# Seven-product groups in the last piece's down projection, 37 of them in the up projection, and mixer A's values in fp32r

## The chip, the cores and the metric

The kernel runs on one core of a Trainium2 chip. The metric is the device time of one execution, in microseconds. Three runs of the kernel before took 1312.78, 1313.6 and 1313.22 us; their median is 1313.22.

## The reference

One layer of a hybrid diffusion backbone, for 128 context tokens and 128 latent tokens, in fp32, model width 2048. Both token groups use the same weights. Each sub-layer is modulated by shift, scale and gate, which come from a conditioning vector.

```
m = silu(c) @ w_ada + b_ada              -> shift1, scale1, gate1, shift2, scale2, gate2
h = rmsnorm(x)*(1+scale1) + shift1
q,k,v of mixer A (8 heads, 2 kv heads), q,k,v of mixer B (8 heads), gates gA, gB = h @ w_in
oA = softmax(qA kA' + sink) vA           # latent tokens also see 128 cached context keys
oB = softmax(qB kB' + bias) vB           # 2-D neighbourhood, and the cached keys
x = x + gate1*((sig(gA)*(oA @ w_br_a) + sig(gB)*(oB @ w_br_b)) @ w_out)
h2 = rmsnorm(x)*(1+scale2) + shift2
x = x + gate2*(relu(h2 @ w_up)**2 @ w_down)   # 2048 -> 8192 -> 2048
```

The outputs are the two x and the new keys and values. Of these steps the change touches `probs @ vA` of mixer A, `h2 @ w_up`, and the last eighth of the sum over 8192 in `@ w_down`.

## The kernel before, in words

**Products.** An fp32 matmul is done as three fp32r products: with x = xH + xL and w = wH + wL, it is xH wH + xH wL + xL wH. A weight tile of 128 x 1024 (512 KB) is loaded by a DMA on SyncE's queue (`raw`), ScalarE copies the high half into `wH` (helper L112), VectorE subtracts, `wL = raw - wH` (L272), and TensorE does twelve matmuls of 128x512 with it, about half of them for context, half for latent tokens.

**Order.** The kernel records a list of steps, `wsteps`, one per weight tile. `run()` goes through them: for each step it issues the loads that are due (the digits of `RUN` say how many steps ahead), prepares the high and low halves as many steps ahead as `LOOK` says (`AHEAD` for high halves alone), issues the step's matmuls, and then whatever was put behind that step with `at(step, function)`: attention jobs, transposes, sums. On each engine the order is then fixed. SyncE's queue holds loads, transposing DMAs and stores in order. POOL's queue holds DMAs that add to a tile: `minus_plus` (L279) makes a low half by writing -wH with ScalarE and adding the weights from memory, in place of VectorE's subtraction, for the steps that `LO_DMA`, `XL_DMA`, `YL_DMA` list; `T_DMA` lists groups one of whose sums is made in the same way (L1477). Large tiles come from one pool of `GEN` buffers of 128 x 1024 fp32. Accumulators are banks: four in `pacc`, four in `paux`.

**MLP.** It runs in 8 pieces of 1024 hidden columns. A piece is first computed (`up_unit` for piece 0, `up_pair` for the others), then relu, square and transposition, then four down units of 512 output columns, each of four steps with twelve matmuls. They add up in `dsum` from piece to piece; a unit begins with a bank that holds the sum so far (`seed`). In the last piece the units end with the gate, the residual and the store (L1145, L1149, L1583); the very last unit, `last_unit`, ends in smaller parts.

**Seven products.** `up_pair(p)` goes through 8 groups of the inner dimension, two weight tiles each. A group multiplies a 2x2 block of inputs with a 2x2 block of weights. A plain group does the eight block products with 24 matmuls. A group that `FAST[p]` lists does it with seven products (Strassen and Winograd's scheme), 21 matmuls into banks `Q1` to `Q7`; plain groups add to some of the same banks and to `Z`. For a seven-group VectorE and ScalarE form sums of weight blocks and split them all: `XH, XL`, `YB` (both halves), `tH, tL`, `uH, uL`. The sums of inputs, `sH, sL`, are made once, by `fast_stat`. At the end of a pair VectorE adds the banks into the results (L1552).

**Mixer A's values.** `values()` (L991) multiplies the transposed probabilities with v in plain fp32, one matmul of 512 columns (four heads) per block of keys: two jobs of one block (context), two of two blocks (latent). The probabilities are transposed by a DMA and joined again (`probs_join`), for the jobs that `TE` lists by TensorE (L970).

**Constants.** `load_consts` loads the rope table, three norm weights and the sink by five DMAs.

## Time and profile before

| | |
|---|---|
| median of 3 runs | 1313.22 us |
| profiled execution: its own time / its span | 1312.65 us / 1310.8 us |
| TensorE busy (matmul) | 1303.2 us, 6333 records |
| TensorE weight loads, beside the matmuls | 1057.9 us |
| VectorE / ScalarE / GpSimd busy | 1126.5 / 904.5 / 57.4 us |
| DMA | 400.90 MB, 306 GB/s in the mean |
| granted clock of the profiled execution | 0.999 |

The span is that of the instructions in the profile; the 1.85 us between it and the execution's own time lie around them. "Busy" of TensorE counts from a matmul's start to its modelled end, and consecutive ones overlap. Rows of groups read: line, engine, operation, output<-inputs, shapes, count, then busy us and mean ns, then the idle time of the engine ahead of them and what ended it. Rows of a timeline begin with start and duration in us; in square brackets stands the idle time before, with its releaser.

### The profile page before, as it was taken

Reading aid. Unit: us, or ns where it says so; the run is one execution under the profiler, and the core shown is the slowest. Engines: PE = TensorE matmul, PEld = TensorE weight load, DVE = VectorE, ACT = ScalarE, POOL = GpSimd, SP = SyncE. Lnnn points to the kernel's source line nnn. Section 1 sums busy time; section 2 is a strip of 40 time slices with the busy share of each in tenths; the row PEclk is TensorE's granted clock in tenths of the full one; section 3 lists DMA queues with packets and bytes.
Section 4 is the critical chain, followed back from the end, with each engine's and each line's share of the span. In section 5 each row is a group of like instructions: output and inputs, shape, how many; then the busy total and the mean of one; then the engine's idle time right before and its main releaser. Section 6 shows DMA issues by size and latency. Waiting matters only on the chain.

```text
span 1310.8 us, 17957 instructions
## 1 busy us (share of the span) xinstructions
PE 1303.2 (99%) x6333; PEld 1057.9 (81%) x6334; DVE 1126.5 (86%) x1446; ACT 904.5 (69%) x1145; POOL 57.4 (4%) x66
## 2 busy tenths in 40 slices
PE   9999999999999999999999999999999999999998
PEld 4778788788788878888888888888888888888887
DVE  4669799989999899999778998987999998789663
ACT  5635566699865655636786878859779597696980
POOL 0000000332000000000000000000000000000000
PEclk9999999999999999999999999999999999999999
DMA  9999999897999989997599789779977978869593
GB/s 371 408 409 408 400 409 389 346 321 232 271 347 349 386 294 365 359 334 235 205 300 318 204 269 287 275 269 273 322 240 238 362 245 278 301 205 367 193 355 96
DMA packets 170138, 400.90 MB, mean 306 GB/s; under 512 B 71840, under 2 KB 73088, under 8 KB 170048
## 3 DMA queue, kind: packets, MB, share of 16 engines
q1 hardware_dynamic: 165744, 387.36, 82.3%
q0 software_dynamic: 4160, 12.32, 5.0%
q8 instruction: 49, 0.80, 0.2%
q14 instruction: 41, 0.34, 0.1%
q10 hardware_dynamic: 144, 0.08, 0.1%
HBM read 373.97 MB, written 10.80 MB: 294 GB/s over the span
## 4 chain that ended last, share of the span: by engine, by line
PE 98%; ACT 1%; DMA 1%; SPq 0%; issue 0%; DVE 0%; ACTq 0%
PE acc L347 17%; PE acc L348 17%; PE acc L349 17%; PE Q L1421 6%; PE Q L1420 6%; PE Q L1419 6%; PE acc L474 5%; PE acc L475 5%; PE acc L476 5%; PE ps_ada L365 3%; PE ps_S L920 1%; PE Z L1421 1%; PE Z L1420 1%; PE Z L1419 1%; DMA araw<-in_w_pair 1%; PE acc L1225 1%
## 5 line engine op out<-in xcount | busy, mean ns | idle before, releaser
L272 DVE TENSOR_TENSOR wL<-raw,wH 128x1024 fp32r<-128x1024 f32 x377 | 442.7, 1219 | 51.2 <-ACT wH L112 49.0
L112 ACT ACTIVATE wH<-raw 128x1024 fp32r<-128x1024 f32 (+1 forms) x394 | 388.5, 1039 | 62.3 <-DMA raw<-in_w_in 22.6
L474 PE MATMUL acc<-wH,hH 128*128 128x512 f32 x272 | 107.1, 394 | 0.6 <-ACT srow L112 0.6
L475 PE MATMUL acc<-wL,hH 128*128 128x512 f32 x272 | 105.9, 389 | 0.0
L476 PE MATMUL acc<-wH,hL 128*128 128x512 f32 x272 | 105.9, 389 | 0.0
L347 PE MATMUL acc<-wH,hH 128*128 128x512 f32 x252 | 101.2, 402 | 0.0
L348 PE MATMUL acc<-wL,hH 128*128 128x512 f32 x252 | 98.3, 390 | 0.0
L349 PE MATMUL acc<-wH,hL 128*128 128x512 f32 x252 | 98.2, 390 | 0.0
L1685 DVE CUSTOM_DVE_ANT_0 aT<-aT,cB,cols 128x1024 f32<-128x1024 f32 x56 | 71.4, 1283 | 0.6
L1685 DVE CUSTOM_DVE_ANT_0 junk<-aT,cB,cols 128x1024 bf16<-128x1024 f32 x56 | 71.2, 1279 | 0.0
L112 ACT ACTIVATE uH<-raw 128x1024 fp32r<-128x1024 f32 x34 | 36.1, 1062 | 47.4 <-DVE raw L1514 38.2
L474 PEld LDWEIGHTS acc<-wH,hH 128*128 128x128 f32 x272 | 51.0, 188 | 14.2 <-issue 2.9
L476 PEld LDWEIGHTS acc<-wH,hL 128*128 128x128 f32 x272 | 51.1, 188 | 10.8
L475 PEld LDWEIGHTS acc<-wL,hH 128*128 128x128 f32 x272 | 51.1, 188 | 10.2
L347 PEld LDWEIGHTS acc<-wH,hH 128*128 128x128 f32 x252 | 47.4, 188 | 10.6 <-issue 1.0
L348 PEld LDWEIGHTS acc<-wL,hH 128*128 128x128 f32 x252 | 47.4, 188 | 10.5 <-issue 0.7
L349 PEld LDWEIGHTS acc<-wH,hL 128*128 128x128 f32 x252 | 47.3, 188 | 9.9
L112 ACT ACTIVATE tH<-t 128x1024 fp32r<-128x1024 f32 x31 | 32.8, 1058 | 30.4 <-DVE t L1506 26.2
L112 ACT ACTIVATE fTa<-pTa 128x2048 uint16<-128x2048 uint16 x16 | 40.5, 2533 | 1.3 <-DVE gc_g L1685 1.3
L1685 DVE CUSTOM_DVE_ANT_0 aT<-aT,cB,gc_g 128x1024 f32<-128x1024 f32 x32 | 40.7, 1282 | 0.4
L1685 DVE CUSTOM_DVE_ANT_0 junk<-aT,cB,gc_g 128x1024 bf16<-128x1024 f32 x32 | 40.7, 1280 | 0.0
L1562 ACT ACTIVATE up<-up 128x1024 f32<-128x1024 f32 x28 | 29.7, 1062 | 15.4 <-DVE up L1552 14.9
(694 smaller groups left out, 3351.9 us busy)
## 6 DMA issues: line engine op xcount, KB each, us to landing
raw<-in_w_in SPq DMA_DIRECT2D x131, 512.0 KB, 9.0
raw<-in_w_down SPq DMA_DIRECT2D x128, 512.0 KB, 6.8
araw<-in_w_pair SPq DMA_DIRECT2D x80, 512.0 KB, 9.8
raw<-in_w_upF SPq DMA_DIRECT2D x68, 512.0 KB, 6.3
aT<-in_w_gT SPq DMA_DIRECT2D x64, 512.0 KB, 7.1
raw<-in_w_up SPq DMA_DIRECT2D x60, 512.0 KB, 6.8
aT<-in_w_adaT SPq DMA_DIRECT2D x48, 512.0 KB, 8.0
raw<-in_w_out SPq DMA_DIRECT2D x32, 512.0 KB, 7.8
```

The source lines that it names most:

```text
L112: act.activation(out, in_, AF.Copy)
L272: dve.tensor_tensor(st["lo"], st["raw"], st["hi"].bitcast(F32), op=OP.subtract)
L347: pe.matmul(acc[tb], sh, wh[:, k, :], start=f, stop=False, **kw)
L348: pe.matmul(acc[tb], sh, wl[:, k, :], start=False, stop=False, **kw)
L349: pe.matmul(acc[tb], sl, wh[:, k, :], start=False, stop=l, **kw)
L474: pe.matmul(acc[tb], sh, wh[:, k, :], start=kt == 0 and k == 0 and not held and not seeded, stop=False, **kw)
L475: pe.matmul(acc[tb], sh, wl[:, k, :], start=False, stop=False, **kw)
L476: pe.matmul(acc[tb], sl, wh[:, k, :], start=False, stop=last and k == 1 and not hold, **kw)
L1419: pe.matmul(acc, stat[0], hi, start=f, stop=False)
L1420: pe.matmul(acc, stat[0], lo, start=False, stop=False)
L1421: pe.matmul(acc, stat[1], hi, start=False, stop=l)
L1685: dve.tensor_tensor_reduce(out, box["raw"], cB[s, tag], 1.0, dst if second else baT[:, part, fb:fb + 1], OP.mult, OP.add, dst)
```

## The change

Five things, beside the tables.

1. **Last piece, down units 1 and 2.** They become a pair, `down_pair`, in the manner of an up pair: four groups, of which `FAST_D = (0, 3)` are groups of seven, both from the first half of the piece (`a14`); the two plain ones are those of the second half (`a15`). `up_pair` becomes a caller of a general `pair()`. The banks `Q2, Q4, Q3, Z` begin with the sums of the earlier pieces, copied in three steps ahead (`sown`). `up_T` keeps the joined values of these two hidden tiles, and `stat_sums` makes the sums of inputs for both of them, though the groups of seven read those of `a14` alone. A new input, `w_downF`, holds the weights of these two units in the arrangement of the seven products. Gate, residual and stores of both units come after the pair.
2. **`FAST` lists 37 groups in place of 34**: pairs 1, 3 and 7 have one more, so pairs 3 and 7 have six and the others five.
3. **Mixer A's values** are three fp32r products per block. VectorE and ScalarE split v once (`values_split`) and the probabilities of each job (`probs_split`).
4. **`TE` lists one more job**, a latent one of mixer A: its probabilities are transposed on TensorE, eight transposes in place of a DMA.
5. **Constants in two loads**, from one array `consts`. With smaller tiles for small vectors and less memory for DMA descriptors, there are 54 large buffers in place of 53.

The tables that set the order are all new: `RUN`, `LOOK`, `AHEAD`, and the places of attention jobs, transposes and accumulating DMAs (POOL's rise from 26 to 38). One gate tile in place of two goes to memory and back, and seven sums in place of eight. `G2_LEAD`, 2 before and -3 now, puts the last loads of gates and residuals behind the last weight loads.

The diff's core:

```diff
-GEN = 53
-SCRATCH = 4096
+GEN = 54
+SCRATCH = 1024
...
-TE = (('A', 0, 1), ('qA', 1), ('qB', 1))
+TE = (('A', 0, 1), ('A', 1, 1), ('qA', 1), ('qB', 1))
...
-G2_LEAD = 2
+G2_LEAD = -3
...
-FAST = {1: (0, 1, 5, 7), 2: (0, 2, 3, 5, 7), 3: (0, 2, 3, 5, 7), 4: (0, 1, 3, 6, 7), 5: (0, 1, 3, 5, 7), 6: (0, 1, 3, 5, 7), 7: (0, 1, 3, 5, 7)}
+FAST = {1: (0, 1, 2, 3, 7), 2: (0, 2, 3, 6, 7), 3: (0, 1, 2, 3, 5, 7), 4: (0, 2, 4, 5, 7), 5: (0, 3, 5, 6, 7), 6: (0, 1, 3, 4, 7), 7: (0, 1, 2, 4, 6, 7)}
...
+V_AT = 75
+SOW_AT = 3
+FAST_D = (0, 3)
+DS_AT = [-12, -1]
...
+    def values_split():
+
+        t = [G(f"v{x}A", F32R)[:, 0:768].rearrange("p (b g d) -> p b g d", b=3, g=2) for x in "HL"]
+        new = units["kvA", 0][:, :, 256:512].rearrange("p s (g d) -> p s g d", g=2)
+        for b, src in ((slice(0, 2), new), (2, K2["ca"][:, 1])):
+            copy(t[0][:, b], src)
+            dve.tensor_tensor(t[1][:, b], src, t[0][:, b].bitcast(F32), op=OP.subtract)
+        vA["hl"] = t
...
+        def probs_split():
+            if mix == "A":
+                t = [G(f"P{x}", F32R)[:, 0:n // 2].rearrange("p (b h q) -> p b h q", b=nb, h=4) for x in "HL"]
+                split(t[0], t[1], st.pop("PT"))
+                st["PH"] = t
...
             if mix == "A":
+                vh, vl = vA["hl"]
                 for b in range(nb):
-                    pe.matmul(ps, v(0, b), st["PT"][:, b].rearrange("p h q -> p (h q)"), start=b == 0, stop=b == nb - 1)
+                    j = 2 if b else s
+                    for i, (x, y) in enumerate(((vh, 0), (vh, 1), (vl, 0))):
+                        pe.matmul(ps, x[:, j, g, :], st["PH"][y][:, b].rearrange("p h q -> p (h q)"),
+                                  start=b == 0 and i == 0, stop=b == nb - 1 and i == 2)
...
+    def down_pair(n0, n1):
+
+        units = PIECES[last]
...
+        def done(n, u):
+            g, r = gbc["g2", n], x1[n]
+            dve.tensor_tensor(u, u, g, op=OP.mult)
+            dve.tensor_tensor(r, r, u, op=OP.add)
+            for s in range(2):
+                out_dma(n, s)
+
+        def sown():
+            return [(q, dsum[n][:, s, :]) for q, n, s in (("Q2", n0, 0), ("Q4", n0, 1), ("Q3", n1, 0), ("Z", n1, 1))]
+
+        for i, n in enumerate(units):
+            at(len(wsteps) + DS_AT[i], lambda n=n: stat_sums(dH, dL, n, aF.pop(n)))
+        pair(len(PIECES), n0, n1, ("down", last, n0), a["w_down"], 4 * units[0], a["w_downF"], FAST_D, 4, x, sc, done, sown)
...
-        for n in range(4):
-            down_unit(p, n)
+        if p < last:
+            for n in range(4):
+                down_unit(p, n)
+        else:
+            down_unit(p, 0)
+            down_pair(1, 2)
+            down_unit(p, 3)
```

**How the order changes, in three places.** On TensorE, in the input projection, at a job of mixer A's values of two blocks (`hH`, `hL` are the halves of h; before):

```order
L347 MATMUL acc<-wH,hH_261 128x512
L348 MATMUL acc<-wL,hH_261 128x512
L349 MATMUL acc<-wH,hL_262 128x512
L991 MATMUL ps_o<-fTPA_3375,u_kvA_2025 128x512
L991 MATMUL ps_o<-fTPA_3375,cacheA 128x512
L347 MATMUL acc<-wH,hH_261 128x512
```

and a job of one block in the changed kernel, with the new transposes behind it:

```order
L353 MATMUL acc<-wH,hL_761 128x512
L1018 MATMUL ps_o<-PH,vHA 128x512
L1018 MATMUL ps_o<-PL,vHA 128x512
L1018 MATMUL ps_o<-PH,vLA 128x512
L986 MATMUL ps_PT<-ident,prob 128x128 x8
L936 MATMUL ps_S<-fTkB_3439,T_qB_3442 128x128 x4
L351 MATMUL acc<-wH,hH_760 128x512
```

One product per block has become three; the eight transposes (`ps_PT`) stand between values and the scores of mixer B (`ps_S`).

On TensorE in the last piece, where unit 1 began before and the pair begins now. Before, a plain step follows a plain step (`a14`, `a15` are the two halves of the piece):

```order
L348 MATMUL acc<-wL,a15H 128x512
L349 MATMUL acc<-wH,a15L 128x512
L347 MATMUL acc<-wH,a14H 128x512
L348 MATMUL acc<-wL,a14H 128x512
L349 MATMUL acc<-wH,a14L 128x512
```

Now unit 0 is followed by the pair's first group of seven and its first plain group:

```order
L353 MATMUL acc<-wH,a15L 128x512
L1479 MATMUL Q_11617<-XH,a14H 128x512
L1480 MATMUL Q_11617<-XL,a14H 128x512
L1481 MATMUL Q_11617<-XH,a14L 128x512
...
L1479 MATMUL Q_11619<-tH,sH_11324 128x512
L1480 MATMUL Q_11619<-tL,sH_11324 128x512
L1481 MATMUL Q_11619<-tH,sL_11325 128x512
...
L1479 MATMUL Q_11538<-wH,a15H 128x512
L1480 MATMUL Q_11538<-wL,a15H 128x512
L1481 MATMUL Q_11538<-wH,a15L 128x512
```

Between the first and the second triple stand twelve matmuls, into the second free bank of `pacc` and into three of the banks begun with copied sums, so `Q_11619`, the first of the banks that unit 0 used, is written from the 16th matmul on.

On SyncE's queue, the end. Before (`g` and `x1b` are the gate and residual rows of a unit; `x1d` is where the residual was kept):

```order
L243 DMA raw<-in_w_down 128x1024 x4
L1711 DMA g_2_11461<-gr_g_10605 128x512 x2
L1330 DMA x1b_11464<-x1d_6239 128x1024
L243 DMA raw<-in_w_down 128x1024 x2
L1583 DMA out_y_prompt<-x1b_11263 128x512
L1583 DMA out_y_sample<-x1b_11263 128x512
L1711 DMA g_3_11554<-gr_g_10605 128x512 x2
L1330 DMA x1b_11557<-x1d_6258 128x1024
```

Now:

```order
L247 DMA raw<-in_w_downF 128x1024
L247 DMA raw<-in_w_down 128x1024 x3
L1635 DMA out_y_prompt<-x1b_11422 128x512
L1635 DMA out_y_sample<-x1b_11422 128x512
L247 DMA raw<-in_w_down 128x1024
L1798 DMA g_1_11664<-gr_g_10640 128x512 x2
L1364 DMA x1b_11667<-x1d_6275 128x1024
L1798 DMA g_2_11683<-gr_g_10640 128x512 x2
L1364 DMA x1b_11686<-x1d_6289 128x1024
```

The last weight load has moved behind the output stores of unit 0 (`x1b_11422`), and the gate and residual rows of units 1 to 3 have moved behind it.

167 lines of the change are left out of this document (101 added, 66 removed).

## The prediction

> **What bounds the kernel now.** I read the busy times first, then the chain of waits, then what TensorE itself waited for. In the rows of the page below the shares are of the 1310.8 us span; the second row is the chain that ended last, by engine.
>
> ```profile
> PE 1303.2 (99%) x6333; PEld 1057.9 (81%) x6334; DVE 1126.5 (86%) x1446; ACT 904.5 (69%) x1145; POOL 57.4 (4%) x66
> PE 98%; ACT 1%; DMA 1%; SPq 0%; issue 0%; DVE 0%; ACTq 0%
> ```
>
> TensorE is busy for all but 7.6 us, and the chain runs through it. TensorE's list of waits has five entries, none over 1.2 us; the first and the last are these (columns: us in total, times, longest):
>
> ```profile
> PE ps_warm L136 <- DVE wm L129: 1.2, 1, 1.2
> ...
> PE ps_warm L136 <- issue: 0.2, 1, 0.2
> ```
>
> Together they come to 3.3 us, all on lines of the first stage, ahead of anything that the change touches. So from there on the time is the number of TensorE instructions times their pitch. The timeline gives the pitch:
>
> ```profile
> 1186.16 0.39 PE L1419 MATMUL Q<-tH,sH 128*128 128x512 f32 x1
> ...
> 1188.43 0.39 PE L1420 MATMUL Q<-uL,sH 128*128 128x512 f32 x1
> ```
>
> Ten fp32r matmuls of 512 columns lie between these two starts: 2.27/10 = 0.227 us each (the 0.39 is a latency that overlaps the next). VectorE is the engine nearest to taking over. Three stretches show how near, and that the granted clock is full (columns: us, then busy time of PE, PEld, DVE, ACT, POOL with counts, granted clock, DMA share, GB/s):
>
> ```profile
> 310.00:560.00 250.00, 250.00 (x1199) 204.99 (x1198) 240.17 (x325) 164.97 (x207) 0.00 (x0) 1.00 0.95 334
> 1100.00:1190.00 90.00, 90.00 (x399) 74.43 (x398) 78.31 (x87) 70.98 (x81) 2.64 (x4) 1.00 0.77 252
> 1190.00:1290.00 100.00, 100.00 (x443) 82.79 (x442) 69.77 (x72) 74.28 (x86) 2.55 (x3) 1.00 0.81 282
> ```
>
> In the attention stretch VectorE has 9.8 us of idle time in 250, in the last pieces 11.7 in 90, in the last hundred microseconds 30.2.
>
> **The change on TensorE.** Everything that I price as time is a count of TensorE instructions.
>
> First, seven products for eight: 21 matmuls in place of 24 in each group that turns. Three groups of the up products (34 to 37) and two of the last piece's down products turn: 5 x 3 = 15 matmuls fewer, 15 x 0.227 = -3.41 us. The matmuls of the groups of seven have this very shape, so I see no bound to set beside it.
>
> Second, mixer A's values: six plain fp32 products become 18 fp32r ones. Rows of the timeline around a job of one block, and around one of two:
>
> ```profile
> 315.83 1.02 PE L991 MATMUL ps_o<-fTPA,u_kvA 128*128 128x512 f32 x2
> 316.28 0.80 PE L347 MATMUL acc<-wH,hH 128*128 128x512 f32 x1
> 316.92 0.40 PE L348 MATMUL acc<-wL,hH 128*128 128x512 f32 x1
> ...
> 352.96 1.02 PE L991 MATMUL ps_o<-fTPA,u_kvA 128*128 128x512 f32 x2
> 353.82 1.02 PE L991 MATMUL ps_o<-fTPA,cacheA 128*128 128x512 f32 x2
> 354.27 0.79 PE L347 MATMUL acc<-wH,hH 128*128 128x512 f32 x1
> 354.91 0.40 PE L348 MATMUL acc<-wL,hH 128*128 128x512 f32 x1
> ```
>
> From a product's start to the start of the second fp32r matmul behind it (the first one's record starts early) are 1.09 us for one block, 1.95 for two. Less one ordinary pitch: 0.86 and 1.72, so 0.86 per product, and the change of form at both ends lies in it. There are two jobs of each kind: 2 x (0.86 + 1.72) = 5.17 us now; 18 x 0.227 = 4.09 after: -1.08. The bounds: if a change of form of 0.1 (priced below) stayed at each of the four jobs, -0.7; more than -1.1 nothing in these rows allows. I take -1.08, since the new products have the operand types of the ordinary ones.
>
> [...]
>
> Third, eight more transposes on TensorE (the probabilities of one job, until now a transposing DMA):
>
> ```profile
> 309.67 0.39 PE L349 MATMUL acc<-wH,hL 128*128 128x512 f32 x1
> 309.90 0.60 PE L970 MATMUL ps_PT<-ident,prob 128*128 128x128 f32 x4
> 310.25 0.48 PE L347 MATMUL acc<-wH,hH 128*128 128x512 f32 x1
> 310.57 0.40 PE L348 MATMUL acc<-wL,hH 128*128 128x512 f32 x1
> ```
>
> Four of them with the return to fp32r put the stream back by 310.57 - 309.67 - 2 x 0.227 = 0.44 us, 0.11 each. The chain of waits has eight such transposes together elsewhere (start, us, ...), and they come to the same:
>
> ```profile
> 547.28 0.87 PE ps_T L1040 x8
> ```
>
> The new eight stand directly ahead of scores, which change form in any case. I take 8 x 0.11 = +0.88. If 0.2 of the 0.44 is the change of form, it is 8 x 0.06 = 0.5; if one comes on top, 1.1.
>
> Fourth, fewer changes of form: one group of modulation rows joins another, and one attention group joins its neighbour.
>
> ```profile
> 468.02 0.39 PE L349 MATMUL acc<-wH,oLB 128*128 128x512 f32 x1
> 468.34 1.93 PE L365 MATMUL ps_ada<-araw,cpad 128*32 128x256 f32 x32
> 470.20 0.50 PE L347 MATMUL acc<-wH,oHB 128*128 128x512 f32 x1
> 470.54 0.40 PE L348 MATMUL acc<-wL,oHB 128*128 128x512 f32 x1
> ```
>
> The way in costs 0.32 - 0.227 = 0.09, the way out 0.34 - 0.227 = 0.11: 0.2 for this group, and 0.1, one of its two ends, for the other: -0.3, with nothing or twice that as bounds.
>
> Sum: -3.41 - 1.08 + 0.88 - 0.3 = -3.9 us. The profiled execution took 1312.65 us and would take 1308.7; it lies 0.57 below the median 1313.22, so the median becomes 1309.3.
>
> **The change beside TensorE**, priced at nothing, with its cover. These are the durations (busy us, mean ns behind the bar):
>
> ```profile
> L272 DVE TENSOR_TENSOR wL<-raw,wH 128x1024 fp32r<-128x1024 f32 x377 | 442.7, 1219 | 51.2 <-ACT wH L112 49.0 <-issue 2.2
> L1517 DVE TENSOR_TENSOR uL<-raw,uH 128x1024 fp32r<-128x1024 f32 x31 | 38.0, 1225 | 0.8
> L1506 DVE TENSOR_TENSOR t<-raw 128x1024 f32<-128x1024 f32 x31 | 37.8, 1219 | 0.0
> L1510 DVE TENSOR_TENSOR XL<-raw,XH 128x1024 fp32r<-128x1024 f32 x22 | 26.8, 1220 | 5.4 <-ACT XH L112 3.4 <-PE Z L1421 1.9
> L1552 DVE TENSOR_TENSOR up<-up,Q 128x512 f32<-128x512 f32 x35 | 23.4, 685 | 4.7 <-ACT up L112 2.5 <-PE Q L1421 0.8
> L1514 DVE TENSOR_TENSOR raw<-raw 128x512 f32<-128x512 f32 x31 | 21.4, 692 | 1.5
> L1513 DVE TENSOR_TENSOR YB<-raw,YB 128x512 fp32r<-128x512 f32 x25 | 17.2, 686 | 3.0 <-ACT YB L112 3.0
> ```
>
> A group of seven asks VectorE for four whole-width subtractions (XL, t, tL, uL: 4.88) and three half ones (2.07), 6.95 us, against 2 x 1.22 = 2.44 for a plain group: +4.5 each, less where a subtraction is made an accumulating DMA. The low halves of values and probabilities add 2 x 1.22 + 2 x 0.69 + 1.1 = 4.9 us in the attention stretch. That fits into its 9.8 idle; the margin is 4.9, and beyond it each microsecond would be one of TensorE's, since the probabilities' low half stands on VectorE between softmax and values, and everything behind values on TensorE, which works in order, waits with them. ScalarE makes the high halves of all these tiles, and has more room than VectorE in the first two stretches and 25.7 us in the third.
>
> The down pair gives VectorE some 17 us more at the end: two sets of sums (the second, of a15, feeds no product), two groups, eight adds of 0.69 and the final multiply and add at 1.22, less the eight half-width ones that go. The 30.2 us of idle time cover it. What TensorE could meet there is banks. The pair needs two that the unit before holds, from its 16th matmul on, 3.4 us in; VectorE empties them in 1.37 us once the unit is through:
>
> ```profile
> 1295.16 1.37 DVE L1145 TENSOR_TENSOR t<-g,acc 128x512 f32<-128x512 f32 x2 [7.17 <-PE acc L349]
> ...
> 1304.00 0.69 DVE L1145 TENSOR_TENSOR t<-g,acc 128x512 f32<-128x512 f32 x1 [1.31 <-PE acc L1361]
> ```
>
> VectorE has waited 7.17 us there, so it is early. Behind the pair come about 8.4 us of its adds, with the next result due after 1304.00 - 1295.16 = 8.8: nothing late, with 0.4 to spare; if late, some tenths of the tail. On SyncE's queue the last weight load now stands behind unit 0's output stores; it is issued about 3 us into the pair, lands some 7 later, and is needed 17 in. The residual and gate rows behind it are needed after 27. Stores and loads move past nothing else.
>
> On POOL's queue stand 12 more accumulating DMAs:
>
> ```profile
> L279 POOL DMA_DIRECT2D XL<-in_w_upF x10: 866/866/892, 659.7 to 1190.0; - x10
> raw<-in_w_upF SPq DMA_DIRECT2D x68, 512.0 KB, 6.3
> XL<-in_w_upF POOLq DMA_DIRECT2D x10, 512.0 KB, 7.3
> ```
>
> (Above minimum, median and maximum ns of the issue; below KB and median us to landing.) Twelve times 0.87 is nothing on an engine that is 4% busy, and each lands 1 us later than a plain load. [...] The two loads of constants for five, and the 54th weight buffer, lie far ahead of any wait of TensorE.
>
> **The rivals.** *Small waits eat the gain.* The smallest lead of VectorE over TensorE in the last pair with sevens is seen here, in the same product as above:
>
> ```profile
> 1185.76 1.23 DVE L1517 TENSOR_TENSOR uL<-raw,uH 128x1024 fp32r<-128x1024 f32 x1
> ...
> 1187.75 0.39 PE L1420 MATMUL Q<-uL,h20H 128*128 128x512 f32 x1
> ```
>
> It ends at 1186.99, 0.76 us ahead of use. With attention's idle time halved and leads of this size, one or a few waits of a microsecond are possible: 1.4 to 5 us of them in all give 1310.7 to 1314.3. Against it: no wait at all after the first stage now, and the loads' and splits' distances are set anew for the new order. Chance 0.22.
>
> *VectorE becomes the bound in the pairs with six sevens* (the slower side). Such a pair asks 174 x 0.227 = 39.5 us of TensorE and of VectorE 6 x 6.95, less two XL by DMA, + 2 x 2.44 + 7 x 0.69 = 49.0. With five sevens and one XL by DMA it was 177 x 0.227 = 40.2 and 45.7. The excess that VectorE must have done ahead grows from 5.5 to 9.5 us, in two pairs. Where the lead is a bare 0.76 us at the end, all of the added 4 us shows: 2 x 4 - 3.9 = +4.1, so 1317.3. It decides once the preparation cannot start 4 us earlier than now. Against it: behind each pair stand four down units at 10.9 us of TensorE each with some 7 of VectorE, so the preparation can begin earlier if loads and buffers allow, and the window of 1100 to 1190 has 11.7 us idle. Chance 0.11.
>
> [...] 0.02 for either.
>
> **How the numbers follow.** My forecast, TensorE's count alone, has 0.65; its own range is 1308.2 to 1310.6 (the bounds of values, transposes and changes of form come to -0.7 and +0.9, the scatter of the runs shown to 0.4). About 0.2%, 2.6 us, can be told from no change: faster ends at 1310.6, slower begins at 1315.8. Faster: 0.65 and a little of the small waits' lower edge, 0.66. Slower: 0.11 and 0.02 of late transfers, 0.13. Same: the rest, 0.21. The range from 1307.2, where a median 0.4 low and a microsecond better than the lower bounds together would lie, to 1314.3 holds the forecast and the small waits, and leaves out the pairs bound by VectorE.
>
> **What would show it.** Right: TensorE's records 3 fewer 512-column matmuls, busy near 1299, its list of waits unchanged at five entries in the first stage, values at pitch 0.227, four fp32 value jobs gone, span near 1306.9. Wrong: entries "PE Q <- DVE uL" or "<- DVE tL" in pairs 3 and 7 (VectorE bound), "PE ps_o <- DVE PL" between 310 and 380 us (attention), or a wait on accumulating DMAs. A tail longer than 4 us behind TensorE's last matmul would mean that VectorE's final adds came late.

## The result, and the profile after

The changed kernel takes 1330.82 us, the median of six executions from 1329.1 to 1336.85; the kernel before takes 1313.05 in the same sessions. The ratio is 1.0144, with an interval of 1.013 to 1.0157: 18 us slower, where 4 us faster were forecast. Four more executions later lie between 1330.2 and 1337.0. The scatter is itself new: the kernel before stays within 1.0 us over six executions.

The profiled execution took 1336.85 us, the longest of the six and 6 us above the median; what is added up below is of it, with e4's trace (1335.28 us) as the second. Its busy times and its chain of waits:

```profile
PE 1308.2 (98%) x6332; PEld 1059.9 (79%) x6333; DVE 1152.9 (86%) x1483; ACT 925.3 (69%) x1173; POOL 72.6 (5%) x78
PE 88%; DMA 5%; DVE 3%; issue 3%; ACT 1%; SPq 0%; DVEq 0%; ACTq 0%; POOLq 0%
```

TensorE's share of the chain fell from 98% to 88%. VectorE's busy time rose by 26 us; its share of the span is the same 86%. What TensorE waited for (us in total, times, longest):

```profile
PE Q L1480 <- DMA YB<-in_w_upF: 7.2, 2, 4.3
PE acc L479 <- DVE wL L276: 2.6, 1, 2.6
PE acc L351 <- ACT acc L116: 2.4, 3, 1.1
PE ps_ada L369 <- DMA araw<-in_w_pair: 2.0, 2, 1.1
PE ps_sel L387 <- ACT S L116: 1.8, 2, 1.3
PE ps_h L1318 <- DVE h2f L1310: 1.5, 1, 1.5
...
PE Q L1480 <- DVE uL L1546: 0.8, 1, 0.8
```

The five entries of the first stage, 3.3 us, have become thirteen, 22 us in all. 10.4 of them (both waits for YB, the three of "acc <- ACT acc" and the one of uL) lie in the MLP. They name a DMA, VectorE and ScalarE: no single engine is the bound. The forecast's "Q <- DVE uL" shows once, at 725 us in pair 1; pairs 3 and 7 show none.

Where it happens is read from the timeline, by the same matmul in both kernels. The first product of the up projection, in the changed kernel and then in the kernel before (a second trace of it, taken beside the experiments, e19 below):

```profile
642.18 0.39 PE L1274 MATMUL acc<-wH,h20H 128*128 128x512 f32 x1
```

```profile
632.09 0.39 PE L1240 MATMUL acc<-wH,h20H 128*128 128x512 f32 x1
```

and the first product of the last piece's down projection, after and before:

```profile
1288.60 0.39 PE L351 MATMUL acc<-wH,a14H 128*128 128x512 f32 x1
```

```profile
1263.69 0.39 PE L347 MATMUL acc<-wH,a14H 128*128 128x512 f32 x1
```

So the change is 10.1 us late when the MLP begins, another 14.8 us are lost up to the last piece, and from there to the last matmul it gains 1.35: the -1.36 of the down pair's six matmuls.

The 14.8 can be added up from the starts of the products in that stretch, 2786 here and 2795 in e19. Starts that are over 0.5 us apart add 12.2 us to the usual pitch of 0.227, eighteen that are 0.42 to 0.44 apart add 3.6 (all but one come behind the long waits, last section), and small ones 1.1 more than in e19. That is 16.9, less nine products at 0.227, 2.04.

### The profile page after: what moved, and what is told of

Read it like the earlier page. It is cut to its first block, busy times and chain, and to the rows that moved or that the text cites. A ratio compares the mean times of both kernels' runs of the same rounds, so it can differ in the third digit from the quotient of the medians.

```text
span 1335.1 us, 18065 instructions
## 1 busy us (share of the span) xinstructions
PE 1308.2 (98%) x6332; PEld 1059.9 (79%) x6333; DVE 1152.9 (86%) x1483; ACT 925.3 (69%) x1173; POOL 72.6 (5%) x78
## 4 chain that ended last, share of the span: by engine, by line
PE 88%; DMA 5%; DVE 3%; issue 3%; ACT 1%; SPq 0%; DVEq 0%; ACTq 0%; POOLq 0%
PE acc L352 15%; PE acc L351 15%; PE acc L353 15%; PE Q L1480 6%; PE Q L1479 6%; PE Q L1481 6%; PE acc L478 4%; PE acc L479 4%; PE acc L480 4%; PE ps_ada L369 2%; DMA raw<-in_w_in 2%; DVE wL L276 1%; DMA araw<-in_w_pair 1%; DMA YB<-in_w_upF 1%; PE ps_S L936 1%
## 5 line engine op out<-in xcount | busy, mean ns | idle before, releaser
L276 DVE TENSOR_TENSOR wL<-raw,wH 128x1024 fp32r<-128x1024 f32 x365 | 429.1, 1220 | 53.2 <-ACT wH L116 39.4
L116 ACT ACTIVATE wH<-raw 128x1024 fp32r<-128x1024 f32 (+1 forms) x385 | 382.4, 1041 | 120.2 <-DMA raw<-in_w_in 46.0
L116 ACT ACTIVATE uH<-raw 128x1024 fp32r<-128x1024 f32 x39 | 41.4, 1062 | 47.7 <-DVE raw L1566 35.3
L479 PEld LDWEIGHTS acc<-wL,hH 128*128 128x128 f32 x272 | 51.4, 189 | 13.3 <-DVE wL L276 3.0
L480 PEld LDWEIGHTS acc<-wH,hL 128*128 128x128 f32 x272 | 51.5, 189 | 10.9
L1558 DVE TENSOR_TENSOR t<-raw 128x1024 f32<-128x1024 f32 x33 | 40.2, 1218 | 3.8 <-PE acc L352 2.4
L116 ACT ACTIVATE XH<-raw 128x1024 fp32r<-128x1024 f32 x39 | 40.4, 1047 | 3.2 <-DMA raw<-in_w_upF 3.0
L1569 DVE TENSOR_TENSOR uL<-raw,uH 128x1024 fp32r<-128x1024 f32 x33 | 40.4, 1224 | 0.9
## 6 DMA issues: line engine op xcount, KB each, us to landing
raw<-in_w_in SPq DMA_DIRECT2D x131, 512.0 KB, 10.1
araw<-in_w_pair SPq DMA_DIRECT2D x80, 512.0 KB, 10.1
```

The lines of the kernel that those rows point to most:

```text
L116: act.activation(out, in_, AF.Copy)
L276: dve.tensor_tensor(st["lo"], st["raw"], st["hi"].bitcast(F32), op=OP.subtract)
L479: pe.matmul(acc[tb], sh, wl[:, k, :], start=False, stop=False, **kw)
L480: pe.matmul(acc[tb], sl, wh[:, k, :], start=False, stop=last and k == 1 and not hold, **kw)
```

## The experiments

Theory O: the new order of the work (the tables) makes the waits, and the five parts cost nothing beside TensorE. Theory P: the parts load the other engines until TensorE waits, in any order. All runs stand beside the kernel before at 1313.07 to 1313.16. "Late" in this table is the start of the same matmul against the trace e19: the first up product, the first product of the last piece, TensorE's last matmul.

| run | median (range), us | up product | last piece | last matmul |
|---|---|---|---|---|
| the change, profiled execution above | 1330.82 (1329.1 to 1336.85) | +10.1 | +24.9 | +23.6 |
| e4 the change again | 1332.96 (1330.2 to 1337.01) | +10.1 | +23.4 | +22.0 |
| e1 all parts, old order | 1333.64 (1332.65 to 1334.95) | +3.6 | +10.1 | +19.7 |
| e3 as e1, groups of seven at old places | 1331.12 (1330.54 to 1332.34) | +3.8 | +7.6 | +17.5 |
| e2 old parts, new order | 1344.66 (1342.55 to 1345.43) | +15.2 | +32.4 | +32.4 |
| e11 all parts, old order up to the MLP | 1326.42 (1324.94 to 1330.13) | +3.7 | +14.7 | +13.3 |
| e5 two YB by VectorE | 1335.69 (1335.49 to 1338.76) | +10.6 | +23.6 | +22.2 |
| e6 53 buffers, old descriptor memory | 1335.85 (1334.75 to 1336.52) | +11.0 | +22.8 | +21.5 |
| e12 old places of transposes | 1335.78 (1334.15 to 1337.47) | +9.5 | +21.9 | +20.9 |
| e13 loads' distances raised | 1329.84 (1324.57 to 1332.12) | +6.8 | +17.9 | +16.6 |
| e17 old places of dots | 1334.15 (1333.3 to 1335.49) | +10.3 | +23.5 | +22.2 |
| e18 old places of constants | 1332.78 (1329.93 to 1333.06) | +5.7 | +18.0 | +16.6 |
| e9 down pair alone, old order | 1313.40 (1312.38 to 1314.45) | +0.3 | +0.9 | +0.9 |
| e14 as e9, sown earlier | 1312.71 (1312.25 to 1313.48) | +0.3 | +0.3 | -0.8 |
| e15 as e14, no unused sums | 1312.08 (1311.35 to 1312.37) | -0.1 | -0.1 | -1.4 |
| e20 as e15, 53 buffers | 1312.25 (1311.42 to 1312.57) | -0.1 | -0.1 | -1.4 |
| e10 as e9, with values and transposes | 1316.69 (1316.43 to 1317.27) | +3.7 | +3.7 | +3.4 |
| e16 as e15, with values, v split later | 1316.84 (1316.77 to 1316.9) | +4.5 | +4.5 | +3.4 |

### Parts against order: e1, e2, e3, e4

Both kernels have the same 456 steps, so their tables can be exchanged whole. e1 is the changed kernel with thirty tables of the kernel before, e2 the reverse:

```diff
-CONST_AT = [72, 58]
+CONST_AT = [73, 75]
...
-T_PAIR = [[14, 6], [6, 9], [10, 8], [6, 8], [8, 10], [8, 9], [6, 13]]
+T_PAIR = [[14, 4], [6, 9], [8, 8], [5, 8], [8, 9], [5, 10], [6, 12]]
...
-G2_LEAD = -3
+G2_LEAD = 2
```

> The changed kernel with all its five parts (37 groups of seven, down pair, values in fp32r, eight more transposes, two loads of constants, 54 buffers), but with the kernel before's tables of order (loads, preparation, attention jobs, dots, accumulating DMAs, transposing DMAs). Theory O (the new order makes the waits; the parts by themselves cost nothing beside TensorE): TensorE's waits are back to some 3.3 us in the first stage, and the time is 1308.7 to 1311. Theory P (the parts load VectorE, ScalarE and the DMAs until TensorE waits, in whatever order): 1322 to 1332, with waits on wL, YB or acc in the same places as in the changed kernel.

> The kernel before with none of the five parts but with the changed kernel's tables of order. Theory O: the waits come with the tables, 1325 to 1335. Theory P: no waits, 1312.5 to 1313.5.

e3 is e1 with the 34 groups of seven where they were and three more:

```diff
+FAST = {1: (0, 1, 3, 5, 7), 2: (0, 2, 3, 5, 7), 3: (0, 1, 2, 3, 5, 7), 4: (0, 1, 3, 6, 7), 5: (0, 1, 3, 5, 7), 6: (0, 1, 3, 5, 7), 7: (0, 1, 3, 4, 5, 7)}
```

> As the run with all parts in the old order, but the 37 groups of seven are the 34 of the kernel before at their old places in their pairs and three more (pairs 1, 3 and 7). The old tables of accumulating DMAs then meet the groups they were made for. Theory O: 1308.7 to 1310. Theory P: as the run with the new places, 1322 to 1332.

> The changed kernel once more, as it is, beside the others on this chip, for a second trace of it. Waits that come of the order and the loads' lengths stand at the same places with sums within a factor of two: at 222 us (wL), 725 and 863 us (YB by an accumulating DMA) and 1160 us (seeded banks). Waits that are chance of one execution are gone. Its time 1329 to 1332.

Neither theory holds alone. The new order without the parts loses 31.6 us, the parts in the old order lose 18 to 20.5, and both together 18. So an order can't be priced without the parts that it was made with, and the medians can't be added up; the places tell more. Up to the first up product the parts in the old order are 3.6 to 3.8 us late, the same in e1, e3 and e11, and the new order makes 10.1 of it. From there to the last piece e3 loses 3.8, the change 13.2 to 14.8. In the last piece it is the other way round. The new order runs it without a wait, and e3 loses 10 us there (columns as in the lists of waits above):

```profile
PE Q L1479 <- DVE t L1179: 9.2, 1, 9.2
```

This is the wait on banks that the forecast described and found covered. In the old order VectorE's queue has the second group's sums ahead of the emptying of unit 0's banks, and TensorE stands until they are empty.

e4 shows that the change's waits are no chance of one execution: they stand at the same places, each within 1 us, but for the 0.8 us of "Q <- DVE uL", which e4 lacks.

In the MLP those places come with the order. e2, which has none of the parts, waits at the same three as the change: at the end of pair 1 (second row below), in pair 3's first group (first row), and at the first product behind pair 5 (2.0 of the last row's 2.7):

```profile
PE Q L1420 <- DMA YB<-in_w_upF: 3.4, 1, 3.4
PE acc L347 <- ACT up L112: 3.1, 1, 3.1
PE acc L347 <- ACT acc L112: 2.7, 2, 2.0
```

e1 and e3, with the parts and the old order, wait 1.3 us at most at the first two.

### Attention: e10, e9, e16

e9 is the changed kernel with the groups of the kernel before, plain fp32 values, and the old order up to the last piece's first down unit: the tables of digits (LOOK, RUN, AHEAD) are the old ones up to step 440 and the new ones from there.

```diff
-FAST = {1: (0, 1, 2, 3, 7), 2: (0, 2, 3, 6, 7), 3: (0, 1, 2, 3, 5, 7), 4: (0, 2, 4, 5, 7), 5: (0, 3, 5, 6, 7), 6: (0, 1, 3, 4, 7), 7: (0, 1, 2, 4, 6, 7)}
+FAST = {1: (0, 1, 5, 7), 2: (0, 2, 3, 5, 7), 3: (0, 2, 3, 5, 7), 4: (0, 1, 3, 6, 7), 5: (0, 1, 3, 5, 7), 6: (0, 1, 3, 5, 7), 7: (0, 1, 3, 5, 7)}
...
-TE = (('A', 0, 1), ('A', 1, 1), ('qA', 1), ('qB', 1))
+TE = (('A', 0, 1), ('qA', 1), ('qB', 1))
...
-    at(V_AT, values_split)
...
-            if mix == "A":
+            if False:
...
-                    for i, (x, y) in enumerate(((vh, 0), (vh, 1), (vl, 0))):
-                        pe.matmul(ps, x[:, j, g, :], st["PH"][y][:, b].rearrange("p h q -> p (h q)"),
-                                  start=b == 0 and i == 0, stop=b == nb - 1 and i == 2)
+                    pe.matmul(ps, v(0, b), st["PT"][:, b].rearrange("p h q -> p (h q)"), start=b == 0, stop=b == nb - 1)
```

> Down pair alone: the groups of seven in the up products, mixer A's values in plain fp32, the transposes on TensorE and the order of everything up to the last piece's first down unit as in the kernel before; the down pair with the changed kernel's order from there on; the constants' two loads and 54 buffers stay. 6 matmuls fewer: -1.36. Theory O (parts cost nothing if the order around them fits): 1311.5 to 1312. Theory P (the parts by themselves make waits): above 1313.5.

e10 keeps the new values and the transposes:

> As the down pair alone, with mixer A's values in fp32r and the eight transposes more on TensorE, in the kernel before's order. TensorE's sum: -1.36 - 1.08 + 0.88 = -1.6. Theory A (VectorE's 4.9 us more in the attention stretch make TensorE wait there, as in the runs with all parts in the old order, which lost 4.4 us up to 460 us): 1315.5 to 1317. Theory O: 1311 to 1312.

e10 is 3.3 us slower than e9. TensorE did what the sum said, three products at 0.23 us each and no change of form at the ends:

```profile
317.10 0.39 PE L353 MATMUL acc<-wH,hL 128*128 128x512 f32 x1
317.33 0.39 PE L1018 MATMUL ps_o<-PH,vHA 128*128 128x512 f32 x1
317.56 0.39 PE L1018 MATMUL ps_o<-PL,vHA 128*128 128x512 f32 x1
317.78 0.39 PE L1018 MATMUL ps_o<-PH,vLA 128*128 128x512 f32 x1
318.01 0.39 PE L351 MATMUL acc<-wH,hH 128*128 128x512 f32 x1
```

What was lost was lost on VectorE. Its timeline in e10 at the split of v, and in the kernel before at the same place:

```profile
266.46 1.21 DVE L819 TENSOR_REDUCE ssq<-sq 128x8 f32<-128x1024 f32 x1
267.59 0.68 DVE L906 TENSOR_TENSOR vLA<-u_kvA,vHA 128x512 fp32r<-128x512 f32 x1
268.19 0.41 DVE L906 TENSOR_TENSOR vLA<-cacheA,vHA 128x256 fp32r<-128x256 f32 x1
268.53 3.49 DVE L276 TENSOR_TENSOR wL<-raw,wH 128x1024 fp32r<-128x1024 f32 x3
```

```profile
265.90 1.21 DVE L816 TENSOR_REDUCE ssq<-sq 128x8 f32<-128x1024 f32 x1
267.03 4.62 DVE L272 TENSOR_TENSOR wL<-raw,wH 128x1024 fp32r<-128x1024 f32 x4
```

The two new subtractions stand ahead of the weights' low half that TensorE needs next; it stands still for 1.09 us, just their length, and the waits at 337 us (1.24) and before scores (1.5) are of the same kind. The window of the kernel before that would have told it is this one (columns as in the windows above):

```profile
250.00:270.00 20.00, 20.00 (x140) 15.17 (x139) 19.76 (x32) 15.87 (x23) 15.19 (x15) 1.00 1.06 348
310.00:340.00 30.00, 30.00 (x146) 24.96 (x145) 29.20 (x45) 28.16 (x44) 0.00 (x0) 1.00 0.93 263
```

VectorE was idle for 0.24 us of 20 and for 0.8 us of 30 where the work was put. The forecast's 9.8 us of idle time lay elsewhere: its window began at 310 us, behind the split of v. e16 moves that split to a later place, and puts the transposes back to the DMA:

```diff
-V_AT = 75
+V_AT = 79
-TE = (('A', 0, 1), ('A', 1, 1), ('qA', 1), ('qB', 1))
+TE = (('A', 0, 1), ('qA', 1), ('qB', 1))
```

> As e15, with mixer A's values in fp32r, v split at step 79 in place of 75, and the transposes on TensorE as in the kernel before. Theory A (place: at step 75 VectorE has no idle time, so the split of v shows whole; later it has some): the wait of 1.1 us at 268 us is gone; the waits behind the probabilities' low halves at 337 us (1.1) and 345 (1.5) may stay. 1.08 less on TensorE: 1310.6 to 1311.0 if all waits go, 1312 to 1314 if those of the probabilities stay. Theory B (VectorE's sum in the whole stretch decides): as in e10, 3 or more above e15.

The wait at 268 us is gone, and others have grown. TensorE's waits in e16 on VectorE:

```profile
PE acc L352 <- DVE wL L276: 3.2, 4, 1.3
...
PE ps_o L1018 <- DVE PL L120: 0.8, 1, 0.8
```

So it is not that one place: with the split of v at either of the two, VectorE is late for something that TensorE needs. The run is 4.8 us slower than e15, theory B.

It is a matter of the old order all the same. The changed kernel has the same values and transposes in an order made for them. From the product at 268.69 us in e19 (276.08 in the change) to the first product of the branches TensorE takes 183.9 us in e19, 187.8 in e10 and 182.5 in the change. e19 and e10 have a group of modulation rows in that stretch (1.93 us in the forecast's rows) that the change has elsewhere. So the values and transposes cost the change some 0.5 us there, an estimate, and e10 3.9.

### The MLP's waits: e5, e12, e6, e13

The largest wait of the changed kernel, at 725 us in pair 1, can be followed back in its timeline (SP is the issue of the transposing DMA; in brackets the idle time before, with its releaser):

```profile
700.84 7.54 SPq L1090 DMA_TRANSPOSE pTa<-pla  x1
...
717.06 2.53 ACT L116 ACTIVATE fTa<-pTa 128x2048 uint16<-128x2048 uint16 x1 [7.49 <-DMA pTa<-pla]
...
721.23 0.63 ACT L282 ACTIVATE YB<-YB 128x512 fp32r<-128x512 f32 x1
722.27 0.86 POOL L283 DMA_DIRECT2D YB<-in_w_upF  x1 [18.92 <-ACT YB L282]
...
730.31 0.79 PE L1480 MATMUL Q<-YB,h22H 128*128 128x512 f32 x1 [4.34 <-DMA YB<-in_w_upF]
```

The transposing DMA of a hidden tile landed 16 us after its issue, where their median is 4.4. ScalarE stood 7.5 us at the join, everything queued behind it was late, and the DMA that fills YB was issued when TensorE was nearly there. e5 makes this and one other YB on VectorE:

```diff
-YL_DMA = [8, 11, 15, 16, 23, 24, 25, 36, 43, 55, 65, 66]
+YL_DMA = [8, 11, 16, 23, 25, 36, 43, 55, 65, 66]
```

> The changed kernel, but two of its ten accumulating DMAs into YB (pair 1's last group, pair 3's first) are VectorE subtractions of 0.69 us again. TensorE waited 4.3 and 3.0 us for these two transfers, and ran its next 10 to 14 matmuls at 0.43 us in place of 0.227. Theory D (a transfer in that place is late, and the wait is its price): both waits go with their slow stretches, 8 to 10 us less than the changed kernel. Theory Q (what is late is the engine queue ahead of the transfer, ScalarE held by a transposing DMA; VectorE's subtraction stands behind the same): the wait at 725 us stays at 1 us or more and is named DVE YB or ACT YB, and 3 to 6 us are gained, mostly at 863.

Theory Q: the transfer is not what is late. Much the same two places now wait for ScalarE, 3.6 and 2.8 us (the first at the first down product, 1.6 us further on):

```profile
PE acc L351 <- ACT up L116: 3.6, 1, 3.6
PE Q L1479 <- ACT dsum L116: 2.8, 1, 2.8
```

The time is no better, 1335.7. e12 puts the planes, the transposing DMAs and the joins where they were:

```diff
-T_PAIR = [[14, 6], [6, 9], [10, 8], [6, 8], [8, 10], [8, 9], [6, 13]]
+T_PAIR = [[14, 4], [6, 9], [8, 8], [5, 8], [8, 9], [5, 10], [6, 12]]
-P_PAIR = [[6, 0], [1, 2], [1, 2], [1, 3], [0, 3], [3, 6], [1, 4]]
+P_PAIR = [[5, -1], [1, 1], [0, 5], [1, 5], [1, 6], [0, 5], [3, 0]]
...
-P_UP = [5, 5]
-T_UP = [19, 10]
+P_UP = [4, 2]
+T_UP = [13, 11]
```

> The changed kernel with one table group of the MLP as before: the places at which hidden values are put into planes, go through the transposing DMA and are joined again (up pairs and first two up units). Theory T (a transposing DMA, issued behind a full row of loads, lands late, holds ScalarE for 7.5 us, and with it what TensorE waits for at 725 us): that wait of 4 to 6 us with its slow stretch goes, and the wait at 863 us shrinks, 1321 to 1325. Theory V (VectorE and ScalarE are behind there in any case): the waits move, less than 3 us gained.

The wait at 725 us is gone: between the first up product and the first down product e12 loses 0.3 us, the change 5.6 to 7.4. So that the transposing DMA and the join behind it made this wait is shown. The other traces with the change's order in the MLP bear it out. Broadly, the longer this DMA takes from issue to landing, the more is lost over that stretch against e19:

| trace | landing, us | lost, us |
|---|---|---|
| e6 | 4.3 | 0.4 |
| e12 | 6.3 | 0.3 |
| e11 | 11.1 | 1.2 |
| e5 | 12.3 | 3.1 |
| e18 | 13.8 | 3.9 |
| e4 | 14.0 | 5.6 |
| e13 | 15.1 | 5.8 |
| e17 | 15.2 | 5.3 |
| the change | 16.1 | 7.4 |

But the wait at 863 us stays in e12 (2.4 us, for ScalarE's copy of a sum), a new one of 3.8 us comes in the down units of piece 5, just ahead of pair 7 (for a dot product, ahead of the gate rows), and the median is not better. Theory V as to the time.

e6 and e13 try two general causes:

```diff
-GEN = 54
-SCRATCH = 1024
+GEN = 53
+SCRATCH = 4096
```

> The changed kernel with 53 large buffers and the old memory of 4096 for DMA descriptors in place of 54 and 1024. Theory S (the small descriptor memory holds up POOL's transfers): XL and YB land as fast as before (medians 7.3 and 7.2 in place of 8.3 and 7.8), the waits for YB go, 1320 to 1325. Theory O (the order alone): the same waits, and a buffer fewer costs 0 to 5: 1329 to 1336.

XL lands at 8.3 us as in the changed kernel (7.3 before), YB at 7.3 (7.8 there, 7.2 before). The wait at 725 us is gone with the late landing (table), the one at 863 is 2.4 us, but 5.4 us are lost around the first product behind pair 5 in place of 2.3, and the time is no better. Two things were changed at once, so the run doesn't tell them apart; the descriptor memory does not account for the time lost.

e13 is the changed kernel with one table other: each of RUN's 456 digits is the larger of its own and that of the kernel before.

> The changed kernel with each digit of the loads' distance raised to the kernel before's where that is larger, so that no load is issued later than in either. Theory L (weights land late since they are issued late): ScalarE's waits for raw fall, TensorE's waits at 222 us and in the MLP shrink, 5 us or more gained. Theory B (buffers and transposing DMAs decide when a load can start, not the table): within 3 us of the changed kernel, either way.

Three executions, 1324.6 to 1332.1: the median is 1 to 3 us better than the change's two and the trace 5 to 7 us. In that trace the wait at 222 us, in the head, is gone too, and pair 3 loses 2.0 us in place of 4.2. Loads that come late probably have a share in the waits; no run isolates it.

### The head: e11, e17, e18

> The changed kernel, all parts, with the kernel before's order in everything up to the first up product (200 steps: modulation, input projection, attention, branches, output projection) and its own order in the MLP. If the order's price is a sum over places, the first up product starts 4.4 us later than in the kernel before (as in the runs with all parts in the old order) in place of 10.8, the MLP loses its 14.8 as in the changed kernel, and the time is 1324 to 1326. If the waits of the MLP hang on how loads stand when it begins, its part changes by more than 3 us.

e11's diff is that of e1 for the first 200 steps. The head is that of e1. The MLP then loses 10.9 us in place of 13.2 to 14.8, which is 2.3 to 3.9 less, on either side of the 3 us that were to tell. Place by place it is no sum: pair 1 loses 1.2 in place of 5.6 to 7.4, and pair 3 loses 6.2 in place of 4.2 to 4.4.

In the head of the change TensorE's longest wait is at 222 us. e17 puts three tables of VectorE's dot products back, e18 the one of the constants:

```diff
-H_AT = 19
-DOTS1 = [15, 30, 33, ...]
+H_AT = 38
+DOTS1 = [20, 27, 30, ...]
...
-DOTS = [30, 48, 48, 50, 52, ...]
+DOTS = [37, 45, 46, 50, 50, ...]
```

> The changed kernel with the places of VectorE's dot products in the first 200 steps as in the kernel before. In the changed kernel a weight load waits 10.4 us at 206 us for a buffer that such a product holds, and TensorE waits 2.6 us at 222. Theory X (these places make the head's added waits): the first up product starts 4 to 6 us later than in the kernel before in place of 10.8, 1325 to 1328. Theory Y (the dots are one of many): less than 2 us gained or none.

```diff
-CONST_AT = [72, 58]
+CONST_AT = [73, 75]
```

> The changed kernel with the two loads of constants (rope, norms, sink and the cached keys; the bias and its masks on POOL) at the steps of the kernel before (73 and 75 in place of 72 and 58). In the changed kernel POOL's masks run from 206 us on, and VectorE's dots take 1.55 us in place of 1.28 beside them, just ahead of the wait at 222 us. If that slowing or the early loads make the wait, it is under 1 us and 3 to 5 us are gained, 1326 to 1328; if not, 1329 to 1333.

With the dots moved the wait at 222 us shrinks to 0.3 us, but new ones come (1.1 at 242, 2.4 at 264, 1.2 at 485) and the head is as late as before. With the constants moved, in e18's trace, the wait is gone and the first up product is 5.7 us late in place of 10.1. In the change the bias is loaded 17 steps sooner, and the masks that GpSimd makes in it run beside VectorE's dots, 1.55 us each in place of 1.28. The changed kernel:

```profile
207.35 1.41 POOL L798 TENSOR_SCALAR_AFFINE_SELECT bias<-bias 64x384 f32<-64x384 f32 x1
...
211.25 1.55 DVE L1772 CUSTOM_DVE_ANT_0 aT<-aT,cB,cols 128x1024 f32<-128x1024 f32 x1
```

and e18, without the masks there:

```profile
208.71 1.28 DVE L1772 CUSTOM_DVE_ANT_0 aT<-aT,cB,cols 128x1024 f32<-128x1024 f32 x1
```

The slower dots and four subtractions slowed in the same way (5.33 us for 4.63) come to some 2.3 us, an estimate, of the 2.6 us wait. But the wait is also gone in e13, where the masks still run beside slow dots, and nearly gone in e17. So the masks are one condition of it among several. e18's profiled execution is its shortest, 1329.93; the other two, 1332.8 and 1333.1, do not show the gain, so 4 us in the time are not shown.

### The down pair by itself: e14, e15, e19, e20

e9 has TensorE's six matmuls less and no gain. One wait takes nearly all of it, for the copies of the earlier sums into the banks:

```profile
PE Q L1474 <- ACT Q L116: 1.1, 1, 1.1
```

```diff
-SOW_AT = 3
+SOW_AT = 4
```

> The down pair alone, as in the run e9, with the copies of the earlier sums into its banks one step earlier (four ahead of the pair). In e9 TensorE waited 1.1 us for them, just what the pair saves. Without that wait 1312.0 to 1312.4, 0.7 to 1.1 below the kernel before; if the copies at the earlier place hold ScalarE's halves of weights up, 1313 to 1314 as e9.

TensorE's last matmul is 0.8 us earlier than in e19, and the end is hardly so: 5.23 us follow it in place of 4.30. VectorE is now busy without a break from 1283 us up to the last add, which has no idle time ahead of it.

```profile
1307.55 0.41 DVE L1174 TENSOR_TENSOR t<-g,acc 128x256 f32<-128x256 f32 x1
```

e15 leaves out the sums of a15, which feed no product:

```diff
-        for i, n in enumerate(units):
-            at(len(wsteps) + DS_AT[i], lambda n=n: stat_sums(dH, dL, n, aF.pop(n)))
+        at(len(wsteps) + DS_AT[0], lambda n=units[0]: stat_sums(dH, dL, n, aF.pop(n)))
+        at(len(wsteps) + DS_AT[1], lambda n=units[1]: aF.pop(n))
```

> The down pair alone, sown early as in e14, without the sums of a15 that feed no product (four quarter-width sums, a copy and a subtraction). In e14 VectorE has no idle time from 1277.6 us to the end, and the last add comes 0.9 us later behind TensorE's last matmul than in the kernel before. Theory E (VectorE sets the end there, and the 3.9 us of these sums are what is too much): the tail is 4.2 to 4.4 us again, 1311.6 to 1312.0. If the tail stays at 5.2, something else holds the adds, and it is 1312.5 to 1312.9.

```profile
1306.14 0.42 DVE L1174 TENSOR_TENSOR t<-g,acc 128x256 f32<-128x256 f32 x1 [0.56 <-PE acc L1390]
```

VectorE waits for TensorE again, and the gain comes out: 1312.08 against 1313.13, ratio 0.9992 with an interval of 0.9983 to 1.0001. Its eleven executions (1311.35 to 1312.37) all lie below the seventeen of the kernel before (1312.48 to 1313.63); the interval just reaches 1. It is the fastest version of this study, and of the change it keeps the down pair, the constants in two loads and the 54th buffer.

> The kernel before, as it is, for a trace on this chip. All runs so far show a wait of 1.0 to 1.5 us for araw at 18 us that the trace of before lacks. If it is of the chip or the execution, it stands here too, and the runs' first 60 us are to be compared with this trace; if it is of the 54 buffers or the new tables, it is absent here: 1312.5 to 1313.5 either way.

> As e15 (down pair alone, sown early, no unused sums), with 53 large buffers and the old memory for DMA descriptors. If the 54th buffer makes the wait for araw at 18 us, it goes: 1310.8 to 1311.4. If not, as e15, 1311.8 to 1312.4.

The wait of 1.2 us for araw at 18 us stands in the kernel before too (one execution, 1313.34 us), so it belongs to the chip or the execution, and e19 is the trace to compare with. The buffers make no difference: e20 as e15.

## Why the prediction was wrong

**TensorE's sum was right, as far as it can be seen.** The down pair: -1.36 forecast; -1.36 from the last piece's first product to the last matmul in the change, and -1.35 in e15. Values: 0.227 us per product, no change of form. e10 is 3.36 us later than e9 at the first up product, and its three new waits come to 1.09, 1.24 and 1.5, 3.83: without them it would be some 0.5 us earlier, where -0.2 was the sum. The three groups' -2.04 are in the count of products, under 16.9 us of waits and half clock. TensorE's records, 6332 for 6333, fit it too: 15 fewer in the groups, six more for the values (18 in place of 12, since a plain product is two records) and eight transposes.

**The step that failed is "priced at nothing, with its cover".** It failed in two ways.

- *The cover was an average.* "That fits into its 9.8 idle; the margin is 4.9": the idle time of 250 us was set against work that was put at places where 20 us had 0.24 and 30 us had 0.8, the first of them ahead of that window. In the old order the values cost +3.3 us with the transposes (e10) in place of -0.2. The three groups of seven cost +3.8 in the old order, from the first up product to the last piece, in place of -2.0 (e3, against e10's 0.0 over the same stretch). That was the forecast's rival of pairs bound by VectorE, and its sign, but smaller: from pair 7's first product to the first behind it e3 is 1.7 us later than e19 where three products fewer should make it 0.7 earlier, so 2.4 are lost, 2.9 with the down units behind it, where 4 were priced. Pair 3 loses 1.3, and for ScalarE's copy of a sum. In the change's own order the values do find cover, at some 0.5 us.
- *The new order was taken as a help.* "The loads' and splits' distances are set anew for the new order" stood as an argument against small waits, with no row behind it. This is where the change's own loss lies. With the parts, the new order makes the head 10.1 us late in place of 3.7, and loses 13 to 15 up to the last piece in place of 3.8 (e3) or 6.5 (e1); and without the parts (e2) it waits at the same places of the MLP. What of it is shown: a transposing DMA that lands late and holds ScalarE (5 to 7 us at 725 us, e12 and the table of landings). The masks on GpSimd beside VectorE's dots are one condition of the wait at 222 us (4.4 us of the head, in e18's trace alone). The waits at 863 and 1160 us were not settled by any run, nor was what delays the transposing DMA, nor why the order alone loses 31.6 us. Those causes stay open.

**The rivals.** Small waits were the right kind, with the wrong size: 1.4 to 5 us were allowed in all, and three of 2.6 to 4.3 us came, with several of about 1 beside them. The place named for VectorE bound pairs, 3 and 7, shows no such wait in the change: the smallest lead of tL and uL there is 1.3 us. The values did gain: in the forecast's own rows a plain product is two records ("x2") 0.43 us apart, 0.86 us in all, and in e10 the three fp32r products in its place take 0.68 us (317.33 to 318.01 us). No run shows POOL transfers that by themselves make TensorE wait, which the forecast's sum for slower counts at 0.02. What the runs showed in its place: "Q <- DMA YB" is the largest entry, 7.2 us, but the issues into YB take 847 to 867 ns, the one waited for at 725 us was issued late, at 722.27 us, behind ScalarE's 7.49 us of standing at the join, and with this YB made by VectorE (e5) the wait moved to ScalarE, 3.6 us.

**The tail was right in the change and not by itself.** "0.4 to spare" behind the pair: the last add waits 0.56 us for TensorE. In e14, where VectorE comes later to it, the same adds set the end by 0.9 us, and the sums of a15, named in the forecast as feeding nothing, were what was too much (e15).

## What to carry to other kernels

Where one engine is busy for 99% of the span and nothing waits, an edit that takes work off it gains its count only if what the edit adds elsewhere finds room at its very place: take the window of the few tens of microseconds into which it falls, and the instruction behind it on its queue, not the idle time of a stage. An order written out by hand belongs to the work it was made for: a new one is a change of its own, to be measured with the old work in it. Test parts one by one in the old order; here that left 1 us of gain, and one set of sums (those of a15) to leave out.

## What the runs showed of the hardware

**A long wait was paid twice.** After most waits of 2 us or more TensorE ran at half its clock for the next 2 to 5 us: in the changed kernel the granted clock was 0.50 from 226.2 to 229.4, from 728.0 to 734.6 and from 867.9 to 871.1 us. The changed kernel at its wait of 222 us, matmuls and then the granted clock (windows as above; the second one stands behind the wait at 725 us):

```profile
225.81 0.40 PE L480 MATMUL acc<-wH,hL 128*128 128x512 f32 x1
226.04 0.54 PE L478 MATMUL acc<-wH,hH 128*128 128x512 f32 x1
226.38 0.63 PE L479 MATMUL acc<-wL,hH 128*128 128x512 f32 x1
226.81 0.63 PE L480 MATMUL acc<-wH,hL 128*128 128x512 f32 x1
...
229.68 0.39 PE L478 MATMUL acc<-wH,hH 128*128 128x512 f32 x1
```

```profile
225.00:229.70 4.70, 4.70 (x15) 3.65 (x15) 4.70 (x6) 1.55 (x4) 0.00 (x0) 0.64 0.85 281
730.20:734.50 4.30, 4.19 (x10) 3.33 (x11) 3.76 (x5) 4.20 (x5) 0.15 (x1) 0.50 0.03 10
```

The pitch goes from 0.23 to 0.43 us. Over all traces of this study, leaving out one pause of 1.0 us close ahead of a longer one, 57 pauses of 0.7 to 1.9 us between products of 512 columns were followed by none of it, and of 26 pauses of 2.1 to 9.4 us all but three (2.2, 2.2 and 2.8 us) were followed by 5 to 12 such matmuls, which cost 1 to 2.4 us. In the changed kernel they are 24 behind three waits, 4.8 us beside the waits themselves. The length of the pause alone does not decide it: 2.1 us were enough in e12, and 2.8 us did not do it in e18.

**The transposing DMA at 701 us kept the DMA engines busy and moved little.** While it was under way, with loads queued beside it, this is the rate over twenty microseconds from 700 us, in slices of half a microsecond:

```profile
GB/s 291 303 402 401 418 451 410 426 375 398 345 294 218 151 24 33 30 132 99 131 114 63 96 50 272 72 54 239 268 401 377 385 377 410 459 410 418 393 393 401
```

For some 7 us the rate is 24 to 272 in place of 400. From 707 to 713 us 1505 packets of 256 bytes keep the 16 DMA engines 95% busy and move 0.39 MB; from 714 to 720 us 560 packets of 4096 bytes keep them 97% busy and move 2.3 MB.

**VectorE's dots were slower beside GpSimd's masks**: 1.55 us each in the change and in e13, 1.28 in e18, where the masks run elsewhere. In e18's trace the wait of 2.6 us behind them is gone; e13 has the slow dots without the wait.
